# Two layers of a three-mixer encoder on one core: the mixers finished in the order B, C, A, the top-64 selection beside the work queue, one rotary pass for both token tiles, and full rows in a product with an odd head

## The chip, the cores and the metric

One core of a Trainium2 chip runs the whole program. The metric is device time in microseconds (us): the median of several executions, and beside it one execution that was profiled. All data is float32. Weight products run on TensorE as three matmuls in a rounded format (fp32r): high part by high part, and the two cross terms.

## What is computed

256 tokens of width 1024 pass two layers. Each layer does, cut to what matters here:

```python
h = rmsnorm(x, norm1_g) * (1 + sc1) + sh1        # sc, sh, g from c @ ada_w, one vector a layer
proj = h @ w_in + b_in                           # 1024 -> 6733 columns
# A: 6 heads. rotary on q, k and on the indexer's q (8 heads) and k (1 head);
#    scores = sum over 8 indexer heads of relu(q.k) * w; the best 64 keys of each query are kept
# B: 5 heads, band attention with a relative-position bias
# C: 5 heads, causal attention with a cumulative log forget gate as bias
y = g0 * (oA @ wA) + g1 * (oB @ wB) + g2 * (oC @ wC)   # g: sigmoid gates from proj, 3 x 1024 columns
x = x + g1_ada * (y @ w_out)
x = x + g2_ada * swiglu(rmsnorm(x, norm2_g) * (1 + sc2) + sh2)
```

A final RMSNorm follows. Rotary turns the first 16 of a head's 64 columns.

## The kernel before

**Tiling.** Tokens are two tiles of 128 (`T = 2`). `h` lies transposed in SBUF as a high and a low part (`hT`). The input projection is cut into 15 column blocks (`IN_BLOCKS`): `qi` (indexer queries), `kwv` (indexer key, indexer weights, A's values), `fb`, `fc`, `f4` (B's and C's queries and keys, feature-major), `qa`, `ka`, `vb`, `vf` (values of B and C, and the forget logits), and six gate blocks `g0` to `g5`, two for each mixer. In layer 0 the first four blocks are multiplied while the program starts, in layer 1 the first two at the end of layer 0; the mixer begins with their evacuation.

**Weights.** SyncE loads 1 MB units; ScalarE rounds each piece of two 128-row groups to the high part (`whi`, L185), VectorE subtracts to get the low part (`wlo`, L186); six pieces are held ahead of TensorE. Between the weights stand units of `ada_w`, which VectorE multiplies and reduces (`ada_mac`, L332). After every fourth vector of a gate, `ada_mac` yields 3000 and then makes TensorE transpose it into a row (`grow`, L351).

**Order.** All engines get their instructions from one Python pass. Its clock (`clock[0]`, "units" below, meant as ns) moves with `beat`: each matmul group adds its estimated length, and every beat advances the generators that are due. `urgent` holds evacuations and `ada_mac`; `queue` holds the attention work, of which at most `WINDOW = 2` generators are active, and a `None` in it waits until none is. The steps are `idx_head` (a score product, relu, and VectorE's weighted sum into `sc`), `topk` (eight times MAX8 and MATCH_REPLACE8 for each token tile, on VectorE, L685 and L686), `load_rel` (B's bias table by DMA), `forget` (C's cumulative sum), and `pair` for two heads: two score products, bias, maximum and logits on VectorE (L751), exponential on ScalarE, normalisation, `yield 7000`, transposes (L769), `yield 1500`, the product with the values (L776). In the loop over the blocks, `at[name]` is queued after a block. `drain` beats without block work until a mixer's output is there; then `branch` multiplies it by `w_branch`, gates it and adds it to `y`.

The order before is `qi kwv fb fc qa ka f4 vb vf g0 g1 | branch A | g2 g3 | branch B | g4 | branch C, half | g5 | branch C, half`. A's pairs stand right after the selection in the queue.

**PSUM.** Four buffers (`ps_gemm`) serve the blocks, and four (`ps_x`) everything small: scores, transposes, value products, the `grow` rows. A buffer is free when its reader is done.

**Rotary.** `rope` is four GpSimd instructions (L540 to L543) for one token tile; `evac` of `qi`, `kwv`, `qa`, `ka` calls it twice. `kwv` then copies the key beside itself (L594), and `to_pairs` transposes the results (L554) after a yield of 6000 (`kwv`: 5000).

**The odd head.** B and C have five heads. Three chunks of 128 rows hold them; in the third, rows 0 to 63 of `oh` are head 4's high part, rows 64 to 127 its low part, and the weights of head 4 stand in both halves. The last product takes 64 rows only:

```python
nc.tensor.matmul(pf, wh[:, fs], oh[:, c], ...)             # L808
nc.tensor.matmul(pf, wl[:HD, fs], oh[:HD, c], ...)         # L809, HD = 64
```

Of the kernel before, what the change touches and what calls it, by code (L numbers as in the profile page):

```python
# [11 lines left out]
F32 = mybir.dt.float32  # L12
# [6 lines left out]
P = 128  # L19
D = 1024  # L20
S = 256
T = 2
# [20 lines left out]
def _span(*pairs):  # L43
# [9 lines left out]
    ("fc", _span((O_C, 256), (O_C + W_BC, 256))),  # L53
    ("qa", _span((O_QA, W_A))),
    ("ka", _span((O_KA, W_A))),
# [3 lines left out]
] + [(f"g{j}", _span((O_G + 512 * j, 512))) for j in range(6)]  # L59
BY_FEATURE = [n for n, _ in IN_BLOCKS if n[0] in "fg"]  # L60
# [32 lines left out]
def hybrid_encoder(ctx: ExitStack, tc: tile.TileContext, a):  # L93
# [124 lines left out]
    clock = [0.0]  # L218
    queue, active, urgent = [], [], []

# [20 lines left out]
    def drain(flag=None):  # L241
        while (queue or active or urgent) if flag is None else not flag():
            beat(1000.0)
# [83 lines left out]
    def ada_mac(l, u, r):  # L327
# [192 lines left out]
    def mixer(l, ap, first):  # L520
# [9 lines left out]

        def rope(view, t):
            H = view.shape[1]
            xr = view[:, :, 0:ROT]
            ta = ap.tile([P, 8, ROT], F32, tag="ra", name="ra")[:, :H]
            tb = ap.tile([P, 8, ROT], F32, tag="rb", name="rb")[:, :H]

            def bc(v):
                return v[:, None, :].to_broadcast([P, H, v.shape[1]])

            nc.gpsimd.tensor_tensor(ta, xr, bc(cc[:, t]), op=OP.mult)  # L540
            nc.gpsimd.tensor_tensor(tb[:, :, :HALF], xr[:, :, HALF:], bc(nsn[:, t]), op=OP.mult)
            nc.gpsimd.tensor_tensor(tb[:, :, HALF:], xr[:, :, :HALF], bc(sn[:, t]), op=OP.mult)
            nc.gpsimd.tensor_tensor(xr, ta, tb, op=OP.add)  # L543

        def to_pairs(src, width, dst, scale):
            n = -(-width // P)
            for p0 in range(0, n, 2):
                m = min(2, n - p0)
                ps = ps_x()
                for j in range(m):  # L550
                    c = (p0 + j) * P
                    w = min(P, width - c)
                    for t in range(T):
                        nc.tensor.transpose(ps[:w, j * S + t * P:j * S + (t + 1) * P], src[t][:, c:c + w], ident)  # L554
                full = [j for j in range(m) if (p0 + j + 1) * P <= width]
                if full:
                    f = len(full)
                    nc.scalar.activation(dst[:, p0:p0 + f, :].rearrange("p a b -> p (a b)"), ps[:, :f * S],
                                         AF.Copy, scale=scale)
                if len(full) < m:  # L560
                    w = width - (p0 + m - 1) * P
                    nc.scalar.activation(dst[:w, p0 + m - 1, :], ps[:w, (m - 1) * S:m * S], AF.Copy, scale=scale)
                yield 1000

        def biased(ps, w, b):
            out = []
            for t in range(T):
                pr = ap.tile([P, 512], F32, tag="pr", name="pr", bufs=4)
                nc.vector.tensor_add(pr[:, :w], ps[t], b)
                out.append(pr)  # L570
            return out

        def heads(v, H):
            return v.rearrange("p (h d) -> p h d", d=HD)

        def evac(name, w, ps, b):
            if name == "qi":
                pr = biased(ps, w, b)
                for t in range(T):
                    rope(heads(pr[t][:, :512], 8), t)  # L580
                yield 6000
                st["qi"] = ap.tile([P, 5, S], F32, tag="qiW", name="qiT", bufs=1)[:, :4]
                yield from to_pairs(pr, 512, st["qi"], 1.0)
            elif name == "kwv":
                kk = []
                st["wi"] = ap.tile([P, T, 8], F32, name="wi", bufs=1)
                st["va"] = ap.tile([P, T, W_A], F32, name="va", bufs=1)
                for t in range(T):
                    pr = ap.tile([P, P], F32, tag="k2", name="k2")
                    nc.vector.tensor_add(pr[:, :72], ps[t][:, :72], b[:, :72])  # L590
                    nc.vector.tensor_scalar(st["wi"][:, t], pr[:, HD:HD + 8], 8 ** -0.5 * 64 ** -0.5, None,
                                            op0=OP.mult)
                    rope(heads(pr[:, :HD], 1), t)
                    nc.gpsimd.tensor_copy(pr[:, HD:], pr[:, :HD])  # L594
                    kk.append(pr)
# [4 lines left out]
                yield from to_pairs(kk, P, st["ki"], 1.0)  # L600
            elif name in ("qa", "ka"):
                pr = biased(ps, w, b)
                for t in range(T):
                    rope(heads(pr[t][:, :W_A], H_A), t)
                yield 6000
                dst = ap.tile([P, 3, S], F32, name=name[0] + "aT", bufs=1)
# [69 lines left out]
        def topk(t):  # L676
# [6 lines left out]
            for i in range(TOPK // 8):  # L683
# [45 lines left out]
        def pair(br, hs):  # L729
            while br == 2 and ("done", 0) not in st:  # L730
                yield 0
# [63 lines left out]
        def branch(br, cb):  # L795
# [4 lines left out]
            for f in range(4):  # L800
                pf = ps[f // 2][:, (f % 2) * S:(f % 2 + 1) * S]
                for c in range(3):
# [3 lines left out]
                    else:  # L806
                        fs = slice(f * P, (f + 1) * P)
                        nc.tensor.matmul(pf, wh[:, fs], oh[:, c], start=False, stop=False, skip_group_check=True)  # L808
                        nc.tensor.matmul(pf, wl[:HD, fs], oh[:HD, c], start=False, stop=True, skip_group_check=True)  # L809
                if f % 2:  # L810
                    i = f // 2
                    yi = y[cb][:, i * 512:(i + 1) * 512]
                    if br == 0:
# [4 lines left out]
                    if (br, cb) == (2, 1):  # L818
                        split_y(1, i)
# [3 lines left out]
        at = {  # L823
            "kwv": [None] + [(idx_head, h) for h in range(8)] + [None, (topk, 0), (topk, 1)],
            "ka": [None, (load_rel,)] + [(pair, 0, (h, h + 1)) for h in (0, 2, 4)] + [None],
            "vb": [None] + [(pair, 1, h) for h in ((0, 1), (2, 3), (4,))] + [None],
            "vf": [None, (forget,), None] + [(pair, 2, h) for h in ((0, 1), (2, 3), (4,))] + [None],
        }
        bias = {0: bias_row(IN_BLOCKS[0][0], len(IN_BLOCKS[0][1]))}

        for i, (name, cols) in enumerate(IN_BLOCKS):
            w = len(cols)
            if name == "g5":
                drain(lambda: ("o", 2) in st and "g4" in st)
                branch(2, 0)
            if i + 1 < len(IN_BLOCKS):
# [7 lines left out]
            if d is not None:  # L844
                spawn(e, d)
            if name == "g5":
# [5 lines left out]
            if name in ("g1", "g3"):  # L852
                br = int(name[1]) // 2
# [3 lines left out]
                st["done", br] = True  # L857
        drain(lambda: "g5" in st)
        branch(2, 1)
        drain()  # L860
# [90 lines left out]
    def mixer_units(l):  # L951
        ws = []
        for i, (name, _) in enumerate(IN_BLOCKS):
            ws += [in_unit(l, i, kg) for kg in range(2)]
            brs = {"g1": [(0, 0), (0, 1)], "g3": [(1, 0), (1, 1)], "g4": [(2, 0)], "g5": [(2, 1)]}.get(name, [])
            ws += [("w", a["w_branch"], ((l * 3 + br) * 2 + cb) * P * 1536, 3, 512) for br, cb in brs]
# [44 lines left out]
    def scale_biases():  # L1001
        nc.vector.tensor_scalar(bcol[:, :, BCOL["g0"]:], bcol[:, :, BCOL["g0"]:], 0.5, None, op0=OP.mult)
        for f in ("fb", "fc"):
# [156 lines left out]
```

## Time and profile before

| | |
|---|---|
| median of 3 runs | 898.23 us (897.24 to 898.52) |
| the profiled execution | 897.24 us, of which the span of the trace is 895.5 us |
| TensorE busy | 860.4 us (96%), granted clock 0.992 on average |
| VectorE, ScalarE, GpSimd busy | 649.0, 470.7, 70.7 us |
| DMA | 200 MB, 224 GB/s |

The span is the time from the first to the last instruction of the trace; the difference of 1.7 us to the execution's own time lies around it. Busy time of TensorE includes the pipeline's overlap, so the distance between the starts of neighbouring matmuls tells more than their length. The granted clock is 1.00 at 2.4 GHz and 0.50 at 1.2 GHz.

### The profile page before, as it was taken

To read this page: it belongs to the slowest core of one execution; us is meant where nothing else is said; L and a number is where in the kernel's file an instruction comes from. 1 tells how busy PE (TensorE), PEld (TensorE's weight loads), DVE (VectorE), ACT (ScalarE), POOL (GpSimd) and SP (SyncE) were. 2 spreads that over 40 slices of the span, in tenths; PEclk is the share of its full clock that TensorE was granted. 3 is DMA by queue.
4 is the path that set the end of the run, shared out by engine and by line. 5 is a ranking of instruction groups with operands and counts; after the bars stand their busy time and mean duration, and the time that the engine had idled before them with its cause. 6 is when DMAs were issued, how large, how long until landed. Compare 5 with 4: busy or idle time off the path is not lost. (4 is left out here: it accounts for less than half of the span.)

```text
span 895.5 us, 15106 instructions
## 1 busy us (share of the span) xinstructions
PE 860.4 (96%) x5918; PEld 786.0 (88%) x5918; DVE 649.0 (72%) x1280; ACT 470.7 (53%) x779; POOL 70.7 (8%) x134
## 2 busy tenths in 40 slices
PE   2999979999999999999998999999999999999996
PEld 2999878989888999998877998999898799999886
DVE  6996998778777666698376698786867765656734
ACT  5564549536565445364353547764555654445522
POOL 2033200000000000000014040000000000000001
PEclk9999989999999999999999999999999999999998
DMA  9965865854555776589456358556473556636801
GB/s 356 412 266 201 327 216 210 299 201 160 206 188 199 282 257 240 194 341 344 156 197 230 137 187 317 218 207 228 136 276 142 188 212 235 227 104 252 325 34 47
DMA packets 32438, 200.49 MB, mean 224 GB/s; under 512 B 3872, under 2 KB 3888, under 8 KB 13680
## 3 DMA queue, kind: packets, MB, share of 16 engines
q1 hardware_dynamic: 30960, 195.16, 59.3%
q0 software_dynamic: 1264, 4.38, 1.7%
q8 instruction: 46, 0.75, 0.3%
q14 instruction: 24, 0.20, 0.1%
q10 hardware_dynamic: 144, 0.00, 0.0%
HBM read 198.48 MB, written 1.05 MB: 223 GB/s over the span
## 5 line engine op out<-in xcount | busy, mean ns | idle before, releaser
L185 ACT ACTIVATE whi<-raw 128x1024 fp32r<-128x1024 f32 (+5 forms) x300 | 288.5, 975 | 275.5 <-PE ps_g L447 163.0
L186 DVE TENSOR_TENSOR wlo<-raw,whi 128x1024 fp32r<-128x1024 f32 (+5 forms) x300 | 333.2, 1122 | 137.5 <-ACT whi L185 136.9
L446 PE MATMUL ps_g<-hT,whi 128*128 128x256 f32 x1056 | 304.6, 288 | 2.2 <-DVE v_vb L612 1.3
L448 PE MATMUL ps_g<-hT,wlo 128*128 128x256 f32 x1056 | 299.6, 284 | 0.0
L447 PE MATMUL ps_g<-hT,whi 128*128 128x256 f32 x1056 | 299.2, 283 | 0.0
L446 PEld LDWEIGHTS ps_g<-hT,whi 128*128 128x128 f32 x1056 | 200.6, 190 | 8.5 <-issue 8.1
L447 PEld LDWEIGHTS ps_g<-hT,whi 128*128 128x128 f32 x1056 | 200.9, 190 | 1.0 <-issue 0.8
L448 PEld LDWEIGHTS ps_g<-hT,wlo 128*128 128x128 f32 x1056 | 200.2, 190 | 0.3 <-issue 0.3
L332 DVE CUSTOM_DVE_ANT_0 raw<-raw,cond 128x1024 f32<-128x1024 f32 x96 | 115.7, 1221 | 22.8 <-DMA raw<-in_ada_w_dram 22.8
L314 PE MATMUL ps_g<-whi,hT 128*128 128x512 f32 (+4 forms) x320 | 117.3, 370 | 0.9 <-ACT hT L1031 0.9
L315 PE MATMUL ps_g<-wlo,hT 128*128 128x512 f32 (+4 forms) x320 | 116.6, 364 | 1.7 <-DVE wlo L186 1.7
L316 PE MATMUL ps_g<-whi,hT 128*128 128x512 f32 (+4 forms) x320 | 115.3, 364 | 0.0
L314 PEld LDWEIGHTS ps_g<-whi,hT 128*128 128x128 f32 x320 | 60.0, 188 | 10.2 <-issue 1.3
L315 PEld LDWEIGHTS ps_g<-wlo,hT 128*128 128x128 f32 x320 | 60.3, 188 | 9.7 <-DVE wlo L186 2.3
L316 PEld LDWEIGHTS ps_g<-whi,hT 128*128 128x128 f32 x320 | 60.1, 188 | 7.7 <-DVE hT L1032 0.3
L314 PE MATMUL ps_g<-whi,aT 128*128 128x512 f32 (+1 forms) x176 | 66.4, 377 | 0.0
L315 PE MATMUL ps_g<-wlo,aT 128*128 128x512 f32 (+1 forms) x176 | 66.3, 377 | 0.0
L316 PE MATMUL ps_g<-whi,aT 128*128 128x512 f32 (+1 forms) x176 | 66.2, 376 | 0.0
L375 POOL TENSOR_SCALAR var<-sq 128x1 f32<-128x1 f32 x10 | 6.5, 647 | 617.5 <-ACT xn L372 614.4
L314 PEld LDWEIGHTS ps_g<-whi,aT 128*128 128x128 f32 x176 | 33.1, 188 | 6.1
L315 PEld LDWEIGHTS ps_g<-wlo,aT 128*128 128x128 f32 x176 | 33.1, 188 | 6.0
L316 PEld LDWEIGHTS ps_g<-whi,aT 128*128 128x128 f32 x176 | 33.1, 188 | 6.1
(215 smaller groups left out, 1012.8 us busy)
## 6 DMA issues: line engine op xcount, KB each, us to landing
raw<-in_ada_w_dram SPq DMA_DIRECT2D x48, 1024.0 KB, 6.3
raw<-in_w_ffn_in_dram SPq DMA_DIRECT2D x40, 1024.0 KB, 4.8
raw<-in_w_in_dram SPq DMA_DIRECT2D x30, 1024.0 KB, 5.0
raw<-in_w_ffn_out_dram SPq DMA_DIRECT2D x20, 1024.0 KB, 7.1
raw<-in_w_branch_dram SPq DMA_DIRECT2D x12, 768.0 KB, 4.4
raw<-in_w_in_dram SPq DMA_DIRECT2D x16, 512.0 KB, 8.3
raw<-in_w_out_dram SPq DMA_DIRECT2D x8, 1024.0 KB, 4.9
raw<-in_w_in_dram SPq DMA_DIRECT2D x8, 768.0 KB, 5.9
```

Of the source, the lines that this page charges most:

```text
L185: nc.scalar.activation(hi, r, AF.Copy)
L186: nc.vector.tensor_sub(lo, r, hi.bitcast(F32))
L314: nc.tensor.matmul(ps, lh, wh, start=start, stop=False)
L315: nc.tensor.matmul(ps, lh, wl, start=False, stop=False)
L316: nc.tensor.matmul(ps, ll, wh, start=False, stop=stop)
L332: nc.vector.tensor_tensor_reduce(out=wj, in0=wj, in1=cond, scale=1.0, scalar=0.0, op0=OP.mult, op1=OP.add, accum_out=mod[l, name][:, k:k + 1])
L375: nc.gpsimd.tensor_scalar(v, self.sq[:, i:i + 1], EPS if i == 0 else self.v, None, op0=OP.add)
L446: nc.tensor.matmul(ps, wh[:, c], ah, start=first, stop=False, skip_group_check=True)
L447: nc.tensor.matmul(ps, wh[:, c], al, start=False, stop=False, skip_group_check=True)
L448: nc.tensor.matmul(ps, wl[:, c], ah, start=False, stop=stop, skip_group_check=True)
```

## The change

The blocks `qa` and `ka` move behind `vf`, and the gate blocks come as `g2 g3 g4 g5 g0 g1`, so that B is finished first, then C, then A (`BRANCHES`). The selection runs in a list of its own, `aside`, which every beat advances outside the window of two, one token tile after the other; A's pairs wait until it is done. `load_rel` stands behind `select`. `rope` works on both token tiles at once, on one tile `pr`, and the yields behind it are 8000 (`qi`), 10000 (`kwv`) and 7000. The `grow` transposes yield 12000 instead of 3000. The product L809 takes all 128 rows; the rows added multiply the low part of the weights by the low part of head 4.

```diff
-    ("qa", ...), ("ka", ...),                    # ahead of f4
     ("f4", ...), ("vb", ...), ("vf", ...),
-] + [(f"g{j}", ...) for j in range(6)]
+    ("qa", ...), ("ka", ...),
+] + [(f"g{j}", ...) for j in (2, 3, 4, 5, 0, 1)]
+BRANCHES = (1, 2, 0)
...
     def beat(ns):
         clock[0] += ns
         advance(urgent)
+        advance(aside)
...
         if name[0] == "g" and k % 4 == 3:
-            yield 3000
+            yield 12000
...
-        def rope(view, t):
+        def rope(view):
...
-            nc.gpsimd.tensor_tensor(ta, xr, bc(cc[:, t]), op=OP.mult)
+            nc.gpsimd.tensor_tensor(ta, xr, bc(cc), op=OP.mult)
...
             if name == "qi":
                 pr = biased(ps, w, b)
-                for t in range(T):
-                    rope(heads(pr[t][:, :512], 8), t)
-                yield 6000
+                rope(heads(pr))
+                yield 8000
...
+                rope(heads(pr[:, :, :HD]))
+                nc.gpsimd.tensor_copy(pr[:, :, HD:], pr[:, :, :HD])
...
-                yield 5000
+                yield 10000
...
+        def select():
+            def both():
+                for t in range(T):
+                    yield from topk(t)
+                    yield 1500
+                st["selected"] = True
+            aside.append([both(), clock[0]])
+            return
+            yield 0
...
         def pair(br, hs):
-            while br == 2 and ("done", 0) not in st:
+            while br == BRANCHES[2] and ("done", BRANCHES[0]) not in st or br == 0 and "selected" not in st:
                 yield 0
...
-                        nc.tensor.matmul(pf, wl[:HD, fs], oh[:HD, c], start=False, stop=True, skip_group_check=True)
+                        nc.tensor.matmul(pf, wl[:, fs], oh[:, c], start=False, stop=True, skip_group_check=True)
...
         at = {
-            "kwv": [None] + [(idx_head, h) for h in range(8)] + [None, (topk, 0), (topk, 1)],
-            "ka": [None, (load_rel,)] + [(pair, 0, (h, h + 1)) for h in (0, 2, 4)] + [None],
-            "vb": [None] + [(pair, 1, h) for h in ((0, 1), (2, 3), (4,))] + [None],
-            "vf": [None, (forget,), None] + [(pair, 2, h) for h in ((0, 1), (2, 3), (4,))] + [None],
+            "kwv": [None] + [(idx_head, h) for h in range(8)] + [None, (select,), (load_rel,)],
+            "vb": [None] + [(pair, 1, h) for h in ((0, 1), (2, 3), (4,))],
+            "vf": [(forget,), None] + [(pair, 2, h) for h in ((0, 1), (2, 3), (4,))],
+            "ka": [None] + [(pair, 0, (h, h + 1)) for h in (0, 2, 4)] + [None],
         }
...
-            if name == "g5":
-                drain(lambda: ("o", 2) in st and "g4" in st)
-                branch(2, 0)
+            if name == "g1":
+                drain(lambda: ("o", 0) in st and "g0" in st)
+                branch(0, 0)
```

The order after is `qi kwv fb fc f4 vb vf qa ka g2 g3 | branch B | g4 g5 | branch C | g0 | branch A, half | g1 | branch A, half`; the order of the weights in memory follows it.

## Rows read from the trace of the kernel before

**Rows 1.** The page's head, its engines (busy us, share, instructions) and the granted clock in 40 slices of the span.

```profile
span 895.5 us, 15106 instructions
PE 860.4 (96%) x5918; PEld 786.0 (88%) x5918; DVE 649.0 (72%) x1280; ACT 470.7 (53%) x779; POOL 70.7 (8%) x134
PEclk9999989999999999999999999999999999999998
```

**Rows 2.** Who TensorE waited for: us in total, times, longest.

```profile
PE ps_x L351 <- DVE mx L751: 4.6, 1, 4.6
PE ps_x L554 <- POOL k L594: 3.3, 2, 1.8
```

**Rows 3.** TensorE's timeline in a half of branch C of layer 1: start us, length us, line, operation, out and in, rows*columns of the array, shape.

```profile
654.63 0.28 PE L808 MATMUL ps_g<-oh,whi 128*128 128x256 f32 x1
654.84 0.38 PE L809 MATMUL ps_g<-oh,wlo 64*128 64x256 f32 x1
655.14 0.38 PE L446 MATMUL ps_g<-oh,whi 128*128 128x256 f32 x1
...
655.96 0.28 PE L808 MATMUL ps_g<-oh,whi 128*128 128x256 f32 x1
```

**Rows 4.** The same view in branch A of layer 0, where every product has 128 rows; six matmuls of one line each lie between the two rows.

```profile
150.22 0.28 PE L448 MATMUL ps_g<-oh,wlo 128*128 128x256 f32 x1
...
151.06 0.28 PE L446 MATMUL ps_g<-oh,whi 128*128 128x256 f32 x1
```

**Rows 5.** The group of L809 in the whole trace: count, busy us, mean ns, idle before.

```profile
L809 PE MATMUL ps_g<-oh,wlo 64*128 64x256 f32 x32 | 12.2, 381 | 0.0
```

**Rows 6.** TensorE's timeline in layer 0, at the start of block g0 and in g1.

```profile
108.09 0.31 PE L316 MATMUL ps_g<-whi,hT 128*128 128x326 f32 x1
109.73 0.36 PE L446 MATMUL ps_g<-hT,whi 128*128 128x256 f32 x1 [1.34 <-DVE v_vb L612]
...
120.00 0.28 PE L448 MATMUL ps_g<-hT,wlo 128*128 128x256 f32 x1
124.83 1.12 PE L351 MATMUL ps_x<-ident,mg 128*128 128x128 f32 x4 [4.55 <-DVE mx L751]
```

**Rows 7.** Stretches: its bounds, its length, busy us (instructions) of each engine, granted clock, DMA share, GB/s. The first one is from the mixer's first block in layer 0 to the end of vf.

```profile
64.02:108.09 44.07, 43.96 (x300) 41.42 (x298) 33.84 (x73) 24.48 (x43) 16.64 (x36) 1.00 0.73 259
124.80:129.40 4.60, 4.57 (x22) 4.57 (x23) 4.60 (x23) 3.36 (x15) 0.40 (x1) 0.50 0.54 207
488.65:491.20 2.55, 2.55 (x13) 2.55 (x13) 0.00 (x0) 0.39 (x1) 0.59 (x1) 0.50 0.78 316
```

**Rows 8.** TensorE's timeline at the entry to layer 1, in block fb.

```profile
484.66 0.28 PE L448 MATMUL ps_g<-hT,wlo 128*128 128x256 f32 x1
486.79 0.33 PE L554 MATMUL ps_x<-ident,k 128*128 128x128 f32 x1 [1.84 <-POOL k L594]
...
488.65 0.56 PE L446 MATMUL ps_g<-hT,whi 128*128 128x256 f32 x1
```

**Rows 9.** GpSimd's timeline at the same place: the first instruction, three of the rotary on the indexer's key, and the last copy.

```profile
478.93 0.46 POOL L540 TENSOR_TENSOR ra<-pr,cc 128x128 f32<-128x128 f32 x1 [18.27 <-DVE pr L569]
...
481.43 0.22 POOL L540 TENSOR_TENSOR ra<-k,cc 128x16 f32<-128x16 f32 x1
...
483.19 1.22 POOL L540 TENSOR_TENSOR ra<-k,cc 128x16 f32<-128x16 f32 x1
...
488.23 0.24 POOL L594 COPY k<-k 128x64 f32<-128x64 f32 x1
```

**Rows 10.** VectorE's groups from 99 to 135 us, which hold a whole selection and the logits of four heads: line, operation, shape, count | busy us, mean ns | idle before.

```profile
L186 DVE TENSOR_TENSOR wlo<-raw,whi 128x1024 fp32r<-128x1024 f32 x8 | 9.7, 1214 | 0.0
L332 DVE CUSTOM_DVE_ANT_0 raw<-raw,cond 128x1024 f32<-128x1024 f32 x5 | 6.1, 1213 | 0.0
L685 DVE MAX8 m<-sc 128x8 f32<-128x256 f32 x8 | 3.3, 418 | 0.1
L686 DVE MATCH_REPLACE8 sc<-m,sc 128x256 f32<-128x256 f32 x8 | 3.3, 409 | 0.0
L685 DVE MAX8 m<-sc 128x8 f32<-128x128 f32 x8 | 2.3, 284 | 0.0
L686 DVE MATCH_REPLACE8 sc<-m,sc 128x128 f32<-128x128 f32 x8 | 2.2, 276 | 0.0
L751 DVE CUSTOM_DVE_ANT_0 lg<-ps_x,sc 128x256 f32<-128x256 f32 x4 | 1.7, 418 | 0.0
L186 DVE TENSOR_TENSOR wlo<-raw,whi 128x652 fp32r<-128x652 f32 x2 | 1.6, 825 | 0.0
L763 DVE TENSOR_SCALAR lg<-lg,sm 128x256 f32<-128x256 f32 x4 | 1.3, 354 | 0.0
L686 DVE MATCH_VALUE_LOAD sc<-m,sc 128x8 f32 x16 | 1.3, 79 | 0.0
L751 DVE CUSTOM_DVE_ANT_0 lg<-ps_x,sc 128x128 f32<-128x128 f32 x4 | 1.1, 284 | 0.0
...
L754 DVE TENSOR_SCALAR mx<-mx 128x2 f32<-128x2 f32 x4 | 0.7, 184 | 0.0
...
L751 DVE DVE_READ_ACCUMULATOR2_ANT mx<- 128x1 f32 x8 | 0.7, 82 | 0.0
L758 DVE RECIPROCAL sm<-sm 128x2 f32<-128x2 f32 x4 | 0.5, 158 | 0.0
```

More of the change, by code (lines that the diff above doesn't have):

```diff
@@ L58 @@
     ("vf", _span((O_C + 2 * W_BC, 326))),
-] + [(f"g{j}", _span((O_G + 512 * j, 512))) for j in range(6)]
+    ("qa", _span((O_QA, W_A))),
+    ("ka", _span((O_KA, W_A))),
+] + [(f"g{j}", _span((O_G + 512 * j, 512))) for j in (2, 3, 4, 5, 0, 1)]
+BRANCHES = (1, 2, 0)
 BY_FEATURE = [n for n, _ in IN_BLOCKS if n[0] in "fg"]
@@ L218, in hybrid_encoder @@
     clock = [0.0]
-    queue, active, urgent = [], [], []
+    queue, active, urgent, aside = [], [], [], []
     def advance(gens):
@@ L241, in drain @@
     def drain(flag=None):
-        while (queue or active or urgent) if flag is None else not flag():
+        while (queue or active or urgent or aside) if flag is None else not flag():
             beat(1000.0)
@@ L529, in bias_row @@
             return b
-        def rope(view, t):
[L532 to L535, printed above, removed]
+        def rope(view):
+            H = view.shape[2]
+            xr = view[:, :, :, 0:ROT]
+            ta = ap.tile([P, T, 8, ROT], F32, tag="ra", name="ra")[:, :, :H]
+            tb = ap.tile([P, T, 8, ROT], F32, tag="rb", name="rb")[:, :, :H]
             def bc(v):
-                return v[:, None, :].to_broadcast([P, H, v.shape[1]])
-            nc.gpsimd.tensor_tensor(ta, xr, bc(cc[:, t]), op=OP.mult)
-            nc.gpsimd.tensor_tensor(tb[:, :, :HALF], xr[:, :, HALF:], bc(nsn[:, t]), op=OP.mult)
-            nc.gpsimd.tensor_tensor(tb[:, :, HALF:], xr[:, :, :HALF], bc(sn[:, t]), op=OP.mult)
+                return v[:, :, None, :].to_broadcast([P, T, H, v.shape[2]])
+            nc.gpsimd.tensor_tensor(ta, xr, bc(cc), op=OP.mult)
+            nc.gpsimd.tensor_tensor(tb[:, :, :, :HALF], xr[:, :, :, HALF:], bc(nsn), op=OP.mult)
+            nc.gpsimd.tensor_tensor(tb[:, :, :, HALF:], xr[:, :, :, :HALF], bc(sn), op=OP.mult)
             nc.gpsimd.tensor_tensor(xr, ta, tb, op=OP.add)
@@ L553, in to_pairs @@
                     for t in range(T):
-                        nc.tensor.transpose(ps[:w, j * S + t * P:j * S + (t + 1) * P], src[t][:, c:c + w], ident)
+                        nc.tensor.transpose(ps[:w, j * S + t * P:j * S + (t + 1) * P], src[:, t, c:c + w], ident)
                 full = [j for j in range(m) if (p0 + j + 1) * P <= width]
@@ L565, in biased, with heads @@
         def biased(ps, w, b):
-            out = []
+            pr = ap.tile([P, T, 512], F32, tag="pr", name="pr", bufs=2)
             for t in range(T):
[L568 to L574, printed above, removed]
+                nc.vector.tensor_add(pr[:, t, :w], ps[t], b)
+            return pr
+        def heads(v):
+            return v.rearrange("p t (h d) -> p t h d", d=HD)
         def evac(name, w, ps, b):
@@ L584, in evac @@
             elif name == "kwv":
-                kk = []
                 st["wi"] = ap.tile([P, T, 8], F32, name="wi", bufs=1)
                 st["va"] = ap.tile([P, T, W_A], F32, name="va", bufs=1)
+                pr = ap.tile([P, T, P], F32, tag="k2", name="k2")
                 for t in range(T):
[L589 to L595, printed above, removed]
+                    nc.vector.tensor_add(pr[:, t, :72], ps[t][:, :72], b[:, :72])
+                nc.vector.tensor_scalar(st["wi"], pr[:, :, HD:HD + 8], 8 ** -0.5 * 64 ** -0.5, None, op0=OP.mult)
+                rope(heads(pr[:, :, :HD]))
+                nc.gpsimd.tensor_copy(pr[:, :, HD:], pr[:, :, :HD])
                 for t in range(T):
                     nc.vector.tensor_add(st["va"][:, t], ps[t][:, 72:], b[:, 72:])
-                yield 5000
+                yield 10000
                 st["ki"] = ap.tile([P, 1, S], F32, name="kiT", bufs=1)
-                yield from to_pairs(kk, P, st["ki"], 1.0)
+                yield from to_pairs(pr, P, st["ki"], 1.0)
             elif name in ("qa", "ka"):
                 pr = biased(ps, w, b)
-                for t in range(T):
-                    rope(heads(pr[t][:, :W_A], H_A), t)
-                yield 6000
+                rope(heads(pr[:, :, :W_A]))
+                yield 7000
                 dst = ap.tile([P, 3, S], F32, name=name[0] + "aT", bufs=1)
@@ L817, in branch @@
                         nc.vector.tensor_add(yi, yi, g[i])
-                    if (br, cb) == (2, 1):
+                    if (br, cb) == (BRANCHES[2], 1):
                         split_y(1, i)
@@ L845, in mixer @@
                 spawn(e, d)
-            if name == "g5":
+            if name == "g1":
                 for j in range(2):
@@ L857, in mixer @@
                 st["done", br] = True
-        drain(lambda: "g5" in st)
-        branch(2, 1)
+        drain(lambda: "g1" in st)
+        branch(0, 1)
         drain()
```

10 lines of the change are left out of this document (4 added, 6 removed).

## The prediction, as put down before the changed kernel ran

> **What bounds the kernel now.** I read the page's head first: TensorE is busy for 96% of the span, the next engine for 72% [rows 1]. So time can go only where TensorE stands, runs slowly, or does something dear. The second view is TensorE's own waits: two of the three lines that matter lie inside the mixers, 4.6 us for the `grow` transposes and 3.3 us for the transposes of the indexer's key [rows 2]. The third is TensorE's timeline around them, where the distance between starts counts. It shows two holes in layer 0, 108.09 to 109.73 and 120.00 to 124.83 [rows 6], one at the entry to layer 1, 484.66 to 488.65 with two transposes in it [rows 8], and behind the second and the third hole a stretch at granted clock 0.50, the 1.2 GHz level [rows 7]. The fourth is the timeline of a branch, for the product that the change widens [rows 3].
>
> Behind the waits stand two other engines. In layer 0 it is VectorE: from 99 to 135 us it does a whole selection and the logits of four heads [rows 10]; the `grow` transposes need a small PSUM buffer that only the logits of A's heads free, and these stand behind the selection. At layer 1 it is GpSimd: its rotary runs from 478.93 to 488.47 [rows 9], and TensorE's turn to transpose the key comes at 484.78, one step of 0.12 us after its last matmul [rows 8].
>
> **The change part by part.**
>
> *Full rows.* With 64 rows, one feature block of a branch of B or C (eight matmuls) takes 655.96 - 654.63 = 1.33 us: the product starts 0.21 us after its forerunner, the next one 0.30 us after it, the one after that 0.23 us later (655.14 to 655.37 in the same view) [rows 3]. With 128 rows throughout, the same shape keeps a step of (151.06 - 150.22) / 7 = 0.12 us [rows 4], so eight take 0.96 us. The edit saves 0.37 us each time, and there are 32 [rows 5]: 11.8 us. The rows added are there already, in the weights and in `oh`, so no load and no copy is added. The bound from below is the two direct steps alone, 0.21 + 0.30 - 0.24 = 0.27 us, 8.6 us in all; the bound from above is the 11.8 us. I take 11.8, since the period of 1.33 us is measured over the whole block.
> The Trainium skill ("TensorE: Matmul & The Clock Gate", section "Why this matters for your kernels") says that a single matmul with 32 contraction rows takes the same time as one with 128. By that rule the edit would bring nothing and the sum would be 11.8 us longer. The same skill ("TensorEngine Tiling", section "Key Properties") says that a change of the tiling mode drains TensorE, which agrees with the two long steps of 0.21 and 0.30 us around L809; the first rule speaks of one matmul, the row of a stream, so I go by the row.
>
> *Rotary on both tiles, and later transposes.* GpSimd took 9.5 us for 16 rotary instructions, two copies and two bias loads [rows 9]. The merged chain has 8 and one copy. An instruction of twice the size is not shown; between nothing more (0.46 us) and twice (0.92 us) I take 0.73 us for `qi`, from 0.22 us at 16 and 0.46 us at 128 elements [rows 9], that is 2.1 ns an element. Four for `qi` at 0.73 or less, four for the key at about 0.25, the copy and the loads make some 5 to 6 us. But the same 16-element instruction also took 1.22 us [rows 9]; if all nine took that, the chain would last 9 x 1.22 = 11 us plus the loads, 12.2 us. So it ends between 484 and 491 us. TensorE's turn moves too: the key's yield goes from 5000 to 10000 units, and the beats of `fb` (642 each) bring it at 10,272 instead of 5,136 units. The old distance from GpSimd's start was 484.78 - 478.93 = 5.85 us, twice that puts the new turn at about 490.6 us. Only the dearest chain would be late, by under 1 us. What goes is 3.99 us from 484.66 to 488.65 less 0.36 us for three normal steps, 3.6 us, and half of the 2.55 us at clock 0.50 [rows 7, 8], 1.3 us: 4.9 us. Later by this are the indexer heads of layer 1, by 2,568 units, and so the selection; A's logits, which need it, now come at 83,000 units, and the selection ends at 44,500. In layer 0 the yields cost nothing either, since the value blocks' matmuls fill them.
>
> *The order B, C, A, the selection aside, and the later `grow` rows.* I added up the beats of the blocks and the yields for both orders; 1000 units are 44.07 / 33.64 = 1.31 us, from 64.02 (0 units) to 108.09 (33,642 units) [rows 7]. Before, in layer 0: selection at 25,500 to 33,600 units, A's first four heads at 34,300 and 35,600, the `grow` transposes between these and A's transposes at 41,300. After: selection at 28,800 to 49,700, B's first four heads at 29,800, their transposes at 36,900, B needed at 54,200 and ready at 48,400, C ready at 72,200 and needed at 82,400, A ready at 92,100 and needed at 100,400. So no `drain` has to wait, in layer 1 neither (B ready at 54,200, needed at 74,700).
> What the order removes: B's logits do not depend on the selection. The `grow` row, 9000 units later, is no longer due just after four heads have taken all four small buffers. The waits that can go are 1.64 - 0.15 = 1.5 us and 4.83 - 0.12 = 4.7 us [rows 6], and half of 4.60 us at clock 0.50 [rows 7], 2.3 us: 8.5 us.
> What it adds: the selection's 12.4 us of VectorE (3.3 + 3.3 + 2.3 + 2.2 + 1.3) [rows 10] now run beside B's logits, and VectorE serves its queue in order. Behind it wait the splitting of weights (six pieces ahead, hence the cover) and the logits that free small buffers. Between B's first logits and their transposes lie 7000 units, 9.2 us. In these VectorE has four heads, 1.7 + 1.1 + 1.3 + 0.7 + 0.7 + 0.5 = 6.0 us [rows 10], and the running work: 9.7 + 1.6 + 6.1 = 17.4 us over 36 us in which TensorE lost 8.5, so 17.4 / 27.5 = 0.63 us per us, 5.8 us. That is 11.8 against 9.2: TensorE waits 2.6 us somewhere in `g2`. The selection's rounds are traced after these logits, so I put them behind; if they came first (at least four rounds of the narrow tile, 8 x 0.64 = 5.1 us, counted from the same rows), the wait would be 7.7 us. If part of the running work waits instead, it is nothing. I take 2.6, with 0 and 8.5 as ends. The gain is 5.9 us.
>
> *The rest* I cost at nothing: the same bias loads, weights and gates in another order, one small VectorE instruction fewer for the indexer's weights. The cover is TensorE's matmuls; B's bias table, loaded two beats before B's first logits in layer 0, is the one part whose cover is thin.
>
> **Sum.** Against the profiled execution's own time, 897.24 us (1.7 us around the span): 897.24 - 11.8 - 4.9 - 5.9 = 874.6. The median of the runs shown is 1.0 us higher, so I predict 876 us.
>
> **The rivals.**
> 1. *VectorE's wait only moves.* Layer 0 loses as much in `g2` as it lost in `g0` and `g1`. For it: the selection and four heads still meet in one stretch, on an engine with 0.37 us in each us to spare. Against it: B does not need the selection's result. Time: 876 + 5.9 = 882 us.
> 2. *GpSimd's chain stays late*, because merged instructions stretch beside VectorE as the single ones did, and the turn does not move as far as the units say. For it: 0.22 and 1.22 us for one shape [rows 9]. Time: 876 + 4.9 = 881 us.
> 3. *The widened product brings nothing*, because the long steps belong to the place and not to the rows. Against it: branch A in rows 4 has the same place without them. This is also what the skill's rule on few rows would give. Time: 876 + 11.8 = 888 us.
> 4. *Everything goes*: no wait is left in layer 0. Time: 876 - 2.6 = 873 us.
> 5. *Slower: VectorE becomes the bound beside the selection, in both layers.* If TensorE, with its small buffers taken by B's logits, waits out every us of the selection, that is 12.4 us in each layer, and after each wait it runs at half clock as it did before, 2.3 us: 29.4 us. Time: 897.24 - 11.8 - 4.9 - 8.5 + 29.4 + 1.0 = 902 us. It decides from 27 us of new waits on. Against it: in layer 1 the same selection cost TensorE no wait among the lines shown, and the rounds are spread over 20,900 units instead of 8,200.
>
> **Chances and range.** Forecast 0.57; rival 1: 0.19; rival 2: 0.08; rival 3: 0.04; rival 4: 0.07; rival 5: 0.05. All but the last are faster than 898.23 by far more than 0.2% (1.8 us, about what a measurement of this kernel can tell from no change). Of the last I give 0.02 to a wait that happens to balance the gains. So faster 0.95, same 0.02, slower 0.03. The range: below, rival 4 and some small waits of under 2 us, 871; above, the row edit at its lower bound (3.2 us less) together with rival 1 or most of rival 2, 886. The forecast's own spread is 873 to 880.
>
> **What would show it.** Right: L809 with 128 rows and steps of 0.12 us around it; TensorE's wait for `k` L594 gone and no clock of 0.50 near the entry to layer 1; in layer 0 no wait of over 3 us for L351, and B's L751 soon after its scores. Wrong: a new line among TensorE's waits, for L751 or L781 on VectorE or for the bias table, in the stretch of `ka` and `g2`; a new stretch at clock 0.50 there; or a branch of B that still takes 1.33 us for eight matmuls.

## The result, and the profile after

The changed kernel takes 878.3 us (median of 876.12 to 879.46), the kernel before 898.3 us in the same set; the ratio is 0.978, with a 95% interval of 0.976 to 0.980. It is faster by 20.0 us (18.2 to 21.9, as a share of 897.0 us, the median of before in the later sets; all gains below are given so). The profiled execution is the slowest of those shown, 879.46 us, and that of before the fastest of its, so from profile to profile the difference is 17.8 us.

The head of the page after, to be held against [rows 1]: TensorE lost 13 us of busy time, VectorE almost none.

```profile
span 877.8 us, 15056 instructions
PE 847.0 (96%) x5918; PEld 782.7 (89%) x5918; DVE 648.3 (74%) x1278; ACT 470.4 (54%) x779; POOL 56.4 (6%) x100
```

Who TensorE waited for (us in total, times, longest), the answer to [rows 2]: the wait for the key is gone, that of the `grow` transposes (now L354) is less than half, and a line has come that was not there: the transposes of a block's `pr` (L557), for GpSimd.

```profile
PE ps_x L557 <- POOL pr L546: 4.0, 1, 4.0
PE ps_x L354 <- DVE mx L758: 2.0, 1, 2.0
```

TensorE's timeline at the widened product, the answer to [rows 3] (L809 is L816 now): every step is 0.12 us.

```profile
626.67 0.28 PE L451 MATMUL ps_g<-oh,wlo 128*128 128x256 f32 x1
626.79 0.28 PE L815 MATMUL ps_g<-oh,whi 128*128 128x256 f32 x1
626.91 0.28 PE L816 MATMUL ps_g<-oh,wlo 128*128 128x256 f32 x1
627.03 0.28 PE L449 MATMUL ps_g<-hT,whi 128*128 128x256 f32 x1
```

The two holes that are left, in the same view: one in layer 0, inside block `ka`, where [rows 6] had two holes, and the new one in layer 1, behind `ka`.

```profile
104.98 0.33 PE L319 MATMUL ps_g<-whi,hT 128*128 128x384 f32 x1
107.30 0.65 PE L354 MATMUL ps_x<-ident,mg 128*128 128x128 f32 x4 [1.99 <-DVE mx L758]
...
539.91 0.33 PE L319 MATMUL ps_g<-whi,hT 128*128 128x384 f32 x1
544.24 0.66 PE L557 MATMUL ps_x<-ident,pr 128*128 128x128 f32 x4 [4.00 <-POOL pr L546]
```

Stretches (columns as in [rows 7]): behind each hole TensorE runs at clock 0.50, and VectorE works without a gap around the new hole (25.00 us of 25.00).

```profile
108.00:111.40 3.40, 3.40 (x12) 3.40 (x11) 3.31 (x19) 3.40 (x15) 0.46 (x1) 0.50 0.39 133
544.95:548.30 3.35, 3.35 (x16) 3.24 (x15) 3.19 (x9) 0.97 (x2) 0.13 (x1) 0.50 0.90 339
520.00:545.00 25.00, 19.95 (x124) 17.93 (x123) 25.00 (x62) 15.69 (x29) 6.52 (x6) 1.00 0.70 250
```

So layer 0 still loses 2.15 us above a normal step and half of 3.4 us, 3.9 us; layer 1 newly loses 4.2 and 1.7, 5.9 us.

Where the time went, in one ordinary table that also serves the experiments. "First part" runs from the span's start to the first transposes of the stream's norm behind layer 0's mixer, "mixer 1" from the last of these transposes before layer 1's mixer to the first behind it; what lies between is 203.2 to 203.7 us in every kernel. Each is one profiled execution. The gain is from the ratio of all runs.

| kernel | gain us (95%) | first part | mixer 1 |
|---|---|---|---|
| before | | 258.6 | 230.3 |
| the change | 20.0 (18.2 to 21.9) | 246.5 | 225.4 |
| e1 rows alone | 12.4 (10.8 to 14.0) | 252.2 | 224.9 |
| e2 due times alone | 2.0 (0.8 to 3.0) | 259.3 | 228.8 |
| e3 rotary alone | 2.8 (1.8 to 3.9) | 259.3 | 225.9 |
| e4 the change, 64 rows | 7.2 (5.7 to 8.5) | 250.3 | 229.2 |
| e12 all but order and selection | 12.6 (11.4 to 13.9) | 254.4 | 223.1 |
| e11 the change, selection queued | 8.6 (5.7 to 11.5) | 259.2 | 228.6 |
| e8 the change, `grow` early | 14.4 (12.0 to 16.9) | 247.7 | 226.9 |
| e5 the change, table early | 18.6 (17.0 to 20.2) | 246.8 | 224.4 |
| e6 the change, qa and ka late | 19.8 (18.0 to 21.6) | 250.2 | 222.1 |
| e7 both | 17.7 (15.2 to 20.2) | 249.2 | 220.5 |
| e9 the change, half a selection | 24.9 (23.9 to 26.1) | 243.9 | 219.8 |
| e10 the change, late in layer 1 alone | 22.0 (20.8 to 23.1) | 244.5 | 222.4 |

e10 and the changed kernel have the same code in layer 0, and their first parts still differ by 2.0 us: differences of that size in one profile say nothing.

### The profile page after: what moved, and what is told of

It is laid out like the page before. It is cut to its first block, busy times and chain, and to the rows that moved or that the text cites. A ratio compares the mean times of both kernels' runs of the same rounds, so it can differ in the third digit from the quotient of the medians.

```text
span 877.8 us, 15056 instructions
## 1 busy us (share of the span) xinstructions
PE 847.0 (96%) x5918; PEld 782.7 (89%) x5918; DVE 648.3 (74%) x1278; ACT 470.4 (54%) x779; POOL 56.4 (6%) x100
## 4 chain that ended last, share of the span: by engine, by line
PE 81%; DVE 8%; DMA 4%; issue 2%; ACT 2%; POOL 2%; POOLq 0%; DVEq 0%; ACTq 0%
PE ps_g L449 16%; PE ps_g L451 16%; PE ps_g L450 16%; PE ps_g L317 8%; PE ps_g L318 8%; PE ps_g L319 8%; DVE wlo L188 3%; DMA raw<-in_ada_w_dram 3%; PE ps_x L783 1%; PE ps_x L643 1%; PE ps_x L776 1%; PE ps_x L642 1%; DVE raw L335 1%; POOL var L378 1%; PE ps_x L449 1%
## 5 line engine op out<-in xcount | busy, mean ns | idle before, releaser
L188 DVE TENSOR_TENSOR wlo<-raw,whi 128x1024 fp32r<-128x1024 f32 (+5 forms) x300 | 332.7, 1120 | 127.6 <-ACT whi L187 126.9
L187 ACT ACTIVATE whi<-raw 128x1024 fp32r<-128x1024 f32 (+5 forms) x300 | 288.9, 975 | 248.4 <-PE ps_g L450 155.1
L335 DVE CUSTOM_DVE_ANT_0 raw<-raw,cond 128x1024 f32<-128x1024 f32 x96 | 116.5, 1230 | 27.5 <-DMA raw<-in_ada_w_dram 27.5
L317 PE MATMUL ps_g<-whi,hT 128*128 128x512 f32 (+4 forms) x320 | 118.8, 375 | 0.9 <-ACT hT L1038 0.9
L319 PE MATMUL ps_g<-whi,hT 128*128 128x512 f32 (+4 forms) x320 | 116.3, 368 | 0.0
L317 PEld LDWEIGHTS ps_g<-whi,hT 128*128 128x128 f32 x320 | 61.1, 192 | 11.3 <-issue 2.5
L319 PEld LDWEIGHTS ps_g<-whi,hT 128*128 128x128 f32 x320 | 61.1, 191 | 7.6
```

The source lines that it names most:

```text
L187: nc.scalar.activation(hi, r, AF.Copy)
L188: nc.vector.tensor_sub(lo, r, hi.bitcast(F32))
L317: nc.tensor.matmul(ps, lh, wh, start=start, stop=False)
L319: nc.tensor.matmul(ps, ll, wh, start=False, stop=stop)
L335: nc.vector.tensor_tensor_reduce(out=wj, in0=wj, in1=cond, scale=1.0, scalar=0.0, op0=OP.mult, op1=OP.add, accum_out=mod[l, name][:, k:k + 1])
```

## The experiments

**The parts one by one.** e1 takes the kernel before with

```diff
-nc.tensor.matmul(pf, wl[:HD, fs], oh[:HD, c], start=False, stop=True, ...)
+nc.tensor.matmul(pf, wl[:, fs], oh[:, c], start=False, stop=True, ...)
```

> The kernel before with the odd heads' third product over all 128 rows and nothing else changed. Theory: the 32 matmuls of the branches of B and C fall from a step of 0.48 us to the 0.11 us of the 128-row ones, and the time falls by 32 x 0.37 = 11.8 us, to about 886.5 us (by the lower bound of the prediction, 8.6 us, to 889.7). Rival 3 of the prediction: the step lasts as long with 128 rows, because it waits for something other than the row mode; then the time stays at 898 us. A third possibility, that the branch is then held by its weights, would show a value between the two and a new wait of TensorE at the branch's matmuls.

884.6 us, 12.4 us gained, in the two layers 6.4 and 5.4 us; the group of L809 shrinks from the 381 ns of [rows 5] to this:

```profile
L809 PE MATMUL ps_g<-oh,wlo 128*128 128x256 f32 x32 | 8.9, 281 | 0.0
```

Rival 3 falls. e4 takes the same edit back on the changed kernel:

> The changed kernel with the odd heads' third product back on 64 rows and nothing else changed. Theory: the full rows act alone and add to the rest, so this loses the 11.8 us that they gave: about 890 us. The other parts of the change alone would then be worth 8.2 us (898.3 to 890). Rival: the order B, C, A changes what the 64-row product costs, for instance because something else now ends the branch; then the loss is well under 8.6 us and the rest of the change is worth more.

889.2 us; the 64-row product costs 20.0 - 7.2 = 12.8 us there. On either kernel the full rows bring about the same, so their gain adds to the rest.

e2 changes the due times only (qi 6000 to 8000, key 5000 to 10000, qa and ka 6000 to 7000, `grow` 3000 to 12000), e3 the rotary only.

> The kernel before with the changed kernel's later due times alone (8000 for qi, 10000 for the key, 7000 for qa and ka, 12000 for the gates' rows), rotary still one token tile at a time, order A, B, C. Theory: the wait of TensorE at layer 1's entry for the key (3.6 us with a half clock of 1.3 us behind it) is a transpose that comes up too early, so the later due time alone takes it away: about 4.9 us off, 893.5 us, and the gates' rows transposed later add or take under 1 us. Rival: the wait goes only if the GpSimd chain itself is shorter (rotary on both tiles at once); then the wait moves with the transposes to another place and the time stays at 897 to 898 us.

> The kernel before with rotary on both token tiles at once alone, due times and order as before. Theory of the prediction: the merged GpSimd chain is ready earlier, so that the key's wait of 3.6 us at layer 1's entry shrinks, but it does not vanish while the transpose's due time stays; 1 to 4.9 us off, 893.5 to 897 us. Rival: with both tiles in one instruction the first tile's result comes later than before, and the wait of its transpose grows; then the time is 898 us or more.

895.2 and 893.6 us. In both the key's wait at the entry to layer 1 is gone. In e3 almost all of it is won, mixer 1 is 4.4 us shorter. In e2 it is not: TensorE meets a wait later, at ka's transposes, which is the rival's "moves with the transposes".

```profile
533.85 0.27 PE L554 MATMUL ps_x<-ident,pr 128*128 128x128 f32 x1
537.28 0.90 PE L554 MATMUL ps_x<-ident,pr 128*128 128x128 f32 x3 [3.16 <-POOL pr L543]
```

e12 puts rows, rotary and due times together, in the order A, B, C with the selection in the queue:

> The kernel before with the full rows, the rotary on both tiles and the later due times, but in the order A, B, C and with the selection in the queue. Theory: the parts measured singly add, 12.4 + 3.4 + 1.8 us off 897, which gives 879 to 880 us; then the order B, C, A with the selection beside the queue is worth only 1 to 2 us in all, not the 5.9 us of layer 0 that the prediction gives it, because layer 1's new wait takes the most of it back. Rival: the later due times and the shorter rotary do the same thing twice and the sum is 882 to 884 us; then the order is worth 4 to 6 us.

884.8 us: the rows' gain and no more. Rotary and due times bring 12.6 - 12.4 = 0.2 us beside the rows, not the 4.8 of e2 and e3 together (each gain here is good to 1 or 2 us), and the theory of additive parts falls; the order with the selection aside is worth 20.0 - 12.6 = 7.4 us. TensorE's waits in e12 show where the rest went: in layer 1 to the wait for `pr`, here at ka's transposes, in layer 0 to two waits in the place of the long one of [rows 2].

```profile
PE ps_x L554 <- POOL pr L543: 3.5, 1, 3.5
PE ps_g L446 <- DVE fl L609: 2.8, 1, 2.8
PE ps_x L762 <- ACT lg L754: 2.0, 1, 2.0
```

e11 undoes the selection's place, in the changed kernel:

```diff
-            aside.append([both(), clock[0]])
-            return
-            yield 0
+            yield from both()
```

> The changed kernel with the selection back in the queue, ahead of the bias table and of B's heads, where the changed kernel has it beside the queue. Theory: B's heads then start only when the selection's beats are over, some 15 us later, and crowd against B's branch; TensorE waits there for VectorE, 3 to 8 us slower than the changed kernel, 881 to 886 us. Rival: VectorE is the bound of the stretch whichever of the two comes first, and the wait of layer 1 at 540 us goes because the selection is over by then; then 873 to 878 us.

887.9 us (883.9 to 895.5), 11.4 us of gain lost, more than expected. With the selection in the queue the order B, C, A is thus no better than A, B, C: it gains 8.6 us where e12 gains 12.6, and the two intervals barely touch. In the order B, C, A, what pays is that B's logits need not wait for the selection; a kernel with the selection aside in the order A, B, C was not run. Layer 1's wait for `pr` is indeed gone, but layer 0 has one of 3.7 us instead, and others came; in the profile, the slowest of its runs, four stretches at clock 0.50 inside the mixers add up to 30.6 us.

e8 takes the `grow` rows back to a due time of 3000:

> The changed kernel with the gates' rows transposed 3000 after their last part and not 12000, as before the change. Theory: the waits of the gates' transposes in layer 0 at 105 us are of that work only because it stands next on TensorE; taken earlier it leaves the same hole, and the time stays within 1.5 us of 878.3 us. Rival: the later due time keeps those transposes out of the wait for VectorE; undone, the holes of layer 0 come back as in the kernel before, 2 to 5 us slower, 880 to 883 us.

882.9 us, 5.6 us of gain lost: the rival's time, but not its mechanism. In this profile the hole in layer 0 (2.5 us, at 113 us) is about as long as in the changed kernel, so the holes of the kernel before do not come back; the one in layer 1 is 5.2 us. The two profiles differ by 1.2 and 1.5 us in the two parts, so not all of the loss can be seen there. Why the early rows cost time stays open.

**The holes that remain.** My first theory gave each a cause of its own: in layer 0 the bias table, whose DMA was issued at 96.55 us and landed 8.05 us later, just before B's logits use it; in layer 1 a transpose due too soon. e5 gives the table its own buffer and loads it first (the buffers of the rotary's temporaries and of the key cut to one to make room), e6 delays qa and ka, e7 does both:

```diff
-            "kwv": [None] + [(idx_head, h) for h in range(8)] + [None, (select,), (load_rel,)],
+            "kwv": [(load_rel,), None] + [(idx_head, h) for h in range(8)] + [None, (select,)],
...
-                yield 7000
+                yield 14000
```

> The changed kernel with the bias table of B and C in a buffer of its own, loaded ahead of the index heads and not after them (to make room, the rotary's temporaries and the key's have one buffer each). Theory: in layer 0 the wait of the gates' transposes at 105 us (2.15 us above a normal step) and the half clock behind it (1.7 us) come from the table's DMA, which lands 8.05 us after its issue, later than B's first four logits: with the table there early both go, 3.9 us, to about 874.5 us. Rival: VectorE, which adds the table, is late by its own backlog (as the prediction had it for this place); then the wait stays at 1.3 us or more with its half clock, and the time falls by 0 to 1.5 us, 877 to 878 us.

> The changed kernel with the due time of qa's and ka's transposes twice as late (14000, not 7000). Theory: the new wait in layer 1 at 540 us (4.2 us, then 1.7 us at half clock) is a transpose that comes up before VectorE, busy with the selection, and GpSimd behind it have made qa; with the later due time it goes: 5.9 us off, about 872.5 us. Rival: the engines are behind by more than the due time can give, and the wait turns up again at qa's transposes or at A's logits, which need them; then 876 to 878.5 us.

> Both: the bias table in its own buffer and loaded early, and the later transposes of qa and ka. Theory: the two waits are in different layers and have different causes, so their gains add: 3.9 + 5.9 = 9.8 us, about 868.5 us. Rival: VectorE is the bound in either stage and only one of the two moves; then no better than the better of the two alone.

878.8, 877.3 and 880.5 us: none differs from the changed kernel. In e5 the table had landed by 65 us, and the wait is still there (1.58 us). The timelines of e5 say why. The first of B's scores, shown at the top, had left TensorE by 102.1 us. VectorE, shown below, first stood 0.79 us for ScalarE's rounding of a weight (L187); then the first logits (L758) came behind two weight splittings, an addition and a maximum of the selection.

```profile
101.46 0.61 PE L643 MATMUL ps_x<-fb,fb 64*128 64x256 f32 x4
...
103.06 1.23 DVE L188 TENSOR_TENSOR wlo<-raw,whi 128x1024 fp32r<-128x1024 f32 x1 [0.79 <-ACT whi L187]
104.20 0.55 DVE L571 TENSOR_TENSOR pr<-ps_g,bias 128x384 f32<-128x384 f32 x1
104.67 0.28 DVE L681 MAX8 m<-sc 128x8 f32<-128x128 f32 x1
104.87 1.21 DVE L188 TENSOR_TENSOR wlo<-raw,whi 128x1024 fp32r<-128x1024 f32 x1
105.99 0.28 DVE L758 CUSTOM_DVE_ANT_0 lg<-ps_x,relW 128x128 f32<-128x128 f32 x1
...
106.69 0.65 PE L354 MATMUL ps_x<-ident,mg 128*128 128x128 f32 x4 [1.58 <-DVE mx L758]
```

The table's landing was only near in time to the wait. Both kernels reach B's first branch product at the same moment, 147.67 us in the changed kernel, 147.69 in e5 (in e10 145.55), though e5 had the smaller hole and no half clock. e6 wins 3.3 us in mixer 1 and loses 3.7 us in the first part, where a wait for VectorE (L731) of 0.7 us is followed by 10.2 us at half clock:

```profile
142.94 0.41 PE L728 MATMUL ps_x<-ident,F 128*128 128x128 f32 x2 [0.67 <-DVE lg L731]
...
143.40:153.60 10.20, 10.20 (x39) 8.68 (x40) 6.88 (x30) 5.50 (x18) 0.00 (x0) 0.50 0.31 109
```

**Whose backlog it is.** e9 leaves out half of the selection: it takes 32 keys and not 64, so it does not do the whole computation. That takes 12.3 / 2 = 6 us per layer off VectorE and changes nothing else:

```diff
-            for i in range(TOPK // 8):
+            for i in range(TOPK // 16):
```

> The changed kernel with half of the selection: four rounds of the maximum and its replacement for each token tile, not eight, so that 32 and not 64 keys are taken (that part of the computation is left out). It takes 16 rounds of 0.77 us, half of them, some 6 us per layer, off VectorE and touches nothing else. Theory, after the early table and the later transposes gave nothing: VectorE's backlog is the bound of both stretches, busy 46.2 of 47.7 us before B's branch in layer 0, and each hole moved was only a place where it showed; then the waits at 105 us and 540 us both shrink or go and 5 to 10 us are won, 868 to 873 us. Rival: the waits come from the order of the work and the transposes' due times alone; then VectorE only idles more and the time stays within 2 us of 878.3 us.

871.8 us, 4.9 us more gained than by the changed kernel. There is no half clock left in either mixer, the wait for `pr` is gone, that for L758 is 0.9 us. The first stretch below lies before B's branch in layer 0, where VectorE is busy for 46.17 us of 47.67 in the changed kernel; the second is the one shown above. VectorE has room again in both, and TensorE has no gap in the second one:

```profile
100.00:147.67 47.67, 46.77 (x358) 42.74 (x357) 42.02 (x137) 31.48 (x75) 6.90 (x11) 1.00 0.71 253
520.00:545.00 25.00, 25.00 (x169) 23.50 (x169) 20.89 (x42) 17.71 (x31) 8.15 (x10) 1.00 0.80 289
```

The additions that make qa's `pr` (L571) start at 529.0 us, 0.9 us after qa's last matmul at 528.08, and GpSimd's rotary on it, of which the first and the last instruction are shown, is over long before TensorE transposes it:

```profile
530.11 0.60 POOL L543 TENSOR_TENSOR ra<-pr,cc 128x192 f32<-128x192 f32 x1 [6.94 <-DVE pr L571]
...
531.53 0.60 POOL L546 TENSOR_TENSOR pr<-ra,rb 128x192 f32<-128x192 f32 x1
...
537.47 0.60 PE L557 MATMUL ps_x<-ident,pr 128*128 128x128 f32 x4
```

In the changed kernel the additions start at 537.32, 6.6 us after qa's last matmul at 530.70, and GpSimd's rotary only then:

```profile
533.36 1.22 DVE L188 TENSOR_TENSOR wlo<-raw,whi 128x1024 fp32r<-128x1024 f32 x1
534.50 1.22 DVE L335 CUSTOM_DVE_ANT_0 raw<-raw,cond 128x1024 f32<-128x1024 f32 x1
...
537.32 1.02 DVE L571 TENSOR_TENSOR pr<-ps_g,bias 128x384 f32<-128x384 f32 x2
```

So VectorE's backlog makes the hole of layer 1: e9 shows it, by the additions and by mixer 1, which is 5.6 us shorter. For the hole of layer 0 it is argued, from VectorE's queue in e5, and not shown: e9's wait of 0.9 us there is no shorter than that of e7 (0.8 us) and hardly shorter than that of e4 (1.1 us), both with the whole selection, and its first part is only 0.6 us shorter than that of e10.

The theory behind e10 is that the due times set where the backlog shows. It keeps 7000 in layer 0 and has 14000 in layer 1.

> The changed kernel with the later due time of qa's and ka's transposes in layer 1 alone. In the profile with it in both layers, layer 1's mixer was 3.3 us shorter than that of the changed kernel and the first stretch with layer 0's mixer 3.8 us longer. Theory: the two are separate, so that layer 1 alone wins 2 to 3.5 us, 875 to 876 us. Rival: what layer 0 lost was no effect of the due time but differs from one execution to the next; then the time is that of the kernel with both, 877.3 us, or that of the changed kernel.

874.4 us, just under the theory's 875 to 876. The median of the changed kernel is 3.9 us higher, by the ratios 2.0 us, and the two intervals just overlap, so that a gain over the changed kernel is likely and not shown. It has the lowest median of the kernels here that do the whole computation. The wait for `pr` is gone from it; half of its length is back at B's value product, while VectorE is still full from 520 to 545 us (24.94 us). TensorE waits there for ScalarE's L777, and ScalarE had stood 2.31 us for VectorE's L709, after which a table load took 1.28 us:

```profile
537.17 0.21 ACT L710 ACTIVATE fa<-fa 128x10 f32<-128x10 f32 x1 [2.31 <-DVE fa L709]
537.40 1.28 ACT L711 ACT_TABLE_LOAD   x1
...
538.81 0.47 ACT L777 ACTIVATE lg<-ps_x 128x384 f32<-128x384 f32 x1
...
537.09 0.33 PE L319 MATMUL ps_g<-whi,hT 128*128 128x384 f32 x1
539.43 1.41 PE L783 MATMUL ps_x<-lg,v_vb 128*128 128x256 f32 x4 [2.00 <-ACT lg L777]
```

## Why the prediction held, and which steps did not

The forecast was 876 us, 22.2 us below the median, and 20.0 came; 878.3 lies in the forecast's own spread. That the total came so close is in part luck: by the runs, the entry to layer 1 brought 4.7 us less than its term, the order 1.5 us and the rows 0.6 us more than theirs. The three terms, each with the runs that measure it:

*Full rows, 11.8 us.* 12.4 alone on the kernel before, 12.8 as the last part. Right, by the upper of the two bounds: the period of a whole block counts, not the two long steps. The rule of the Trainium skill on few rows ("TensorE: Matmul & The Clock Gate", section "Why this matters for your kernels"), carried over to this stream, would have given 888 us; the runs decide against it for 64-row matmuls in a stream of 128-row ones.

*Order and selection, 5.9 us.* 7.4 from e12 to the changed kernel; in the profiles 7.9 are won in the first part, and mixer 1 loses 2.3. Right in size for layer 0, and so was the remainder, 2.6 us: between 1.5 (e10) and 3.9 us (the changed kernel) with the same code. Its place was not as forecast. The prediction put the wait at B's transposes in `g2`; it lies in `ka`, still at the `grow` transposes, which wait for B's logits (L758). Its doubt about the bias table was unfounded (e5). Two of its side figures are misread: the 5.1 us for "at least four rounds" count eight, four are 2.6 us, and the second of the two bias loads starts at 488.74 us, behind the 9.5 us that it gives for GpSimd. The sum uses neither. The prediction's rival 1, that the wait only moves, is what happens to the order with the selection in the queue (e11, whose first part is 259.2 us, as before the change).

*Entry to layer 1, 4.9 us.* This is the step that failed: 0.2 us are left of it from e1 to e12, and mixer 1, which it was to shorten, is 224.9 us in e1 and 225.4 in the changed kernel. The wait went as forecast, on GpSimd's merged chain: it ran from 466.92 to 472.4 us, 5.5 us, where the forecast had 5 to 6, and the key was transposed at 478.69 without a hole.

```profile
466.92 0.74 POOL L543 TENSOR_TENSOR ra<-pr,cc 128x256 f32<-128x256 f32 x1 [18.92 <-DVE pr L571]
...
471.81 0.56 POOL L531 DMA_DIRECT2D bias<-in_b_row_dram  x1
...
478.56 0.28 PE L451 MATMUL ps_g<-hT,wlo 128*128 128x256 f32 x1
478.69 0.38 PE L557 MATMUL ps_x<-ident,k 128*128 128x128 f32 x2
```

But the gain was kept only in e3 (4.4 us in mixer 1). With the later due times the wait came back at later transposes that need VectorE and then GpSimd: ka's in e2 and e12, qa's in the changed kernel. The sentence that erred is the one that let the selection of layer 1 come 2,568 units later and looked only at A's logits as what could be late: qa's own additions stand in VectorE's queue too, beside a selection whose maxima now start from 499.0 to 531.8 us, so spread over 32.8 us and not 13.4 (513.9 to 527.3 before). Rival 2 named the stretching of GpSimd's instructions, but looked for it at the entry. Of the prediction's signs of being wrong, "a new line among TensorE's waits" came true a layer further on than it looked, and "a new stretch at clock 0.50" both there and in `ka` of layer 0 (108.00 to 111.40), where it had looked. Of its signs of being right, "B's L751 soon after its scores" failed: the scores start at 102.39 us, the first logits (now L758) at 106.61.

*Rival 5*, VectorE as the bound beside the selection, has the right mechanism in the small for layer 1: 5.9 us of TensorE's time, not 12.4 and 2.3. If layer 0's 3.9 us are counted to it as well, which is not shown, its 9.8 us are still less than what the change gives elsewhere.

## To carry to other kernels

A wait that is removed can let the fast engine run ahead until it meets the next place where the slower one is late (e2, e12 and the changed kernel; not e3); so ask of each gain whether the engine behind the wait has room afterwards (its busy share in the stretch, 25.00 us of 25.00 here), not only whether its result comes in time. To tell a backlog from a bad order, take work off the suspected engine without moving anything. And a due time that is right in one layer can be wrong in the other, where the same code meets other neighbours.

## What the hardware showed

GpSimd and VectorE hold each other up. In the changed kernel, the four rotary instructions on qa run beside VectorE's L188 and L335, which read two tensors, and the same four on ka ten us later, while VectorE is idle for 3.02 us; GpSimd first, then VectorE:

```profile
538.42 1.50 POOL L543 TENSOR_TENSOR ra<-pr,cc 128x192 f32<-128x192 f32 x1 [9.58 <-DVE pr L571]
539.89 1.43 POOL L544 TENSOR_TENSOR rb<-pr,nsn 128x96 f32<-128x96 f32 x1
541.29 1.36 POOL L545 TENSOR_TENSOR rb<-pr,sn 128x96 f32<-128x96 f32 x1
542.73 1.45 POOL L546 TENSOR_TENSOR pr<-ra,rb 128x192 f32<-128x192 f32 x1
548.17 0.59 POOL L543 TENSOR_TENSOR ra<-pr,cc 128x192 f32<-128x192 f32 x1 [3.98 <-DVE fl L713]
548.71 0.39 POOL L544 TENSOR_TENSOR rb<-pr,nsn 128x96 f32<-128x96 f32 x1
549.06 0.39 POOL L545 TENSOR_TENSOR rb<-pr,sn 128x96 f32<-128x96 f32 x1
549.53 0.60 POOL L546 TENSOR_TENSOR pr<-ra,rb 128x192 f32<-128x192 f32 x1
...
538.25 1.22 DVE L188 TENSOR_TENSOR wlo<-raw,whi 128x1024 fp32r<-128x1024 f32 x1
...
539.87 1.21 DVE L188 TENSOR_TENSOR wlo<-raw,whi 128x1024 fp32r<-128x1024 f32 x1
541.01 1.40 DVE L335 CUSTOM_DVE_ANT_0 raw<-raw,cond 128x1024 f32<-128x1024 f32 x1
...
551.19 1.23 DVE L188 TENSOR_TENSOR wlo<-raw,whi 128x1024 fp32r<-128x1024 f32 x1 [3.02 <-ACT whi L187]
```

Each took 0.9 to 1.0 us longer, nearly one of VectorE's 1.21 us, and VectorE's L335 took 1.40 instead of 1.22 us. The 0.22 and 1.22 us for one shape in [rows 9], which the prediction's sum took as a spread and its rival 2 put down to VectorE, fit this: in the kernel before, VectorE is idle at the first of the two (481.43 us) and runs L186 at the second (483.19 us).

```profile
483.10 1.23 DVE L186 TENSOR_TENSOR wlo<-raw,whi 128x1024 fp32r<-128x1024 f32 x1 [2.12 <-ACT whi L185]
```

The Trainium skill ("SBUF — State Buffer", section "SBUF: two separate sides") states that the two engines share a pair of ports which one instruction holds to its end, a VectorE instruction with two inputs in SBUF among them; this trace agrees. The chain on qa was 5.8 us long (538.42 to 544.18) and not 2.0, 3.8 us more, and the hole behind it is 4.2 us; but the chain also started late, behind VectorE's additions, and no run here takes away the one without the other. Two estimates from these rows say that either would have done most of it. In e9 the chain starts at 530.11 us, and even 5.8 us long it would have ended before the transposes at 537.47. In the changed kernel a chain of 2.0 us from 538.42 would have ended at 540.4, when TensorE had stood for only some 0.3 us.
